# Three instead of two Strassen pairs in the down projection, and evictions of the gated products at high priority

## The chip, the cores and the metric

The kernel runs on one core of one Trainium2 chip. The time is device time in microseconds (us) of one execution; the lower the better. The kernel before takes 1574.93 us, the median of three runs (1574.7 to 1575.7).

## The reference, cut to what matters

One layer of a gated hybrid block on 256 tokens, model width 2048. All matrices are float32.

```
h = rms_norm(x) ; proj = h @ w_in                      # 2048 -> 12288
y_a, y_b, y_x = three branches, each 1024 wide @ (1024 x 2048)
merged = sum_i sigmoid(gate_i) * y_i                   # gates: 2048 columns of proj each
x = x + rms_norm(merged @ w_o)                         # 2048 x 2048
h = rms_norm(x)
f = square(relu(h @ w_up)) @ w_down                    # 2048 -> 8192 -> 2048
x = x + rms_norm(f)
```

The change touches two places: the product with `w_down` (8192 x 2048), and the step `y_i * sigmoid(gate_i)` that follows each branch's output projection.

## The kernel before

**Products in two parts.** Each float32 number is kept as a high part `wh` (or the first half of an activation tile), rounded to fp32r, and a low part `wl` (what the rounding left out). A product is three matmuls: high by high, high by low, low by high. For each weight tile that is loaded into `raw`, ScalarE makes `wh` (L146, L163, or L168 with a gain) and VectorE subtracts to make `wl` (L147, L164, L169). The tiles `raw` have 6 buffers, `wh` and `wl` 5 each; `in_unit` (L197) fetches four units ahead of the one that TensorE works on (`LOOK`, L48).

**Blocks.** `block` (L286) computes 256 tokens by 1024 columns as four banks of 128 x 512, C11, C12, C21 and C22. A plain k-tile of 128 rows of the weight (a unit called row here, R in short) gives four products, 12 matmuls. Two k-tiles can be taken together as a pair by Strassen's scheme (the form with seven products instead of eight): 21 matmuls instead of 24. A pair j comes as four units, first, second, outer and inner (f, s, o and i in short):

- first j is loaded; only its right half is split, for product P1 (3 matmuls). Then GpSimd issues a DMA that adds its left half onto its right half in place (L149).
- second j is loaded and split (6 matmuls). Then GpSimd issues a DMA that adds its left half onto first's left half (L151).
- outer j is made by VectorE from first and second with two additions (L138, L139), which wait for the DMA of L149 and for second's load, and is split (6 matmuls, banks P6 and C21).
- inner j is the tile of first after both DMAs, split again (6 matmuls, banks Q5 and P7).

The activations that go with them are sums of quarters: `quarter_sums` (L644) for the input and `w_o`, `down_sums` (L921) for the down projection. `plan_rows` (L101) interleaves these units with plain rows. With two pairs and `lead=4` (L403) a down block has 20 units:

```
R R R R f0 R s0 R f1 R o0 R s1 i0 R o1 R i1 R R
```

When the last matmul into P1, P6, P7 and Q5 has been issued, `gathered` adds these four banks into the four sums that C11 to C22 stand for (`gather` L335, or `gather_add` L344 where sums of earlier blocks are there).

**Stages.** The MLP goes through 8192 hidden channels in four parts of 2048 (the loop at L930). Each part has four groups of the up projection (`channels_first`, 128 matmuls a group) and then the down projection: two blocks `n` = 0 and 1 of 1024 columns, or in the last part one such block and two `tokens_first` groups of 512 columns without pairs. So seven blocks have pairs. The hidden channels' sums for the pairs (`down_sums`) are made as groups 0 and 1 of the up projection come out.

**Order.** Instructions are placed by the tile framework's scheduler: each has a priority, `fetch` works at an offset of 400 (`PRIO`), `soon()` (L190) at 800; others go at the priority of their place in the text. The result is one fixed sequence on each engine, in which an instruction waits for its semaphores and those behind it wait with it. PSUM has 8 banks; a new bank is taken from those whose last reader comes first in the program.

**The gated products.** `out_of` (L677) multiplies the four banks of a branch's output by the gates (L684 or L686) and adds them up (L687). After the last one, `turn_merged` transposes the sums on TensorE (L791) for the product with `w_o`, whose block g_o[0] has three pairs (R R f0 s0 f1 o0 s1 i0 R f2 ...).

Of the kernel before, what the change touches and what calls it, by code (L numbers as in the profile page):

```python
# [8 lines left out]
F32 = mybir.dt.float32  # L9
# [6 lines left out]
P = 128  # L16
# [10 lines left out]
NC5 = 512  # L27
# [15 lines left out]
X_PAIRS = ((0, 8), (1, 9), (2, 10))  # L43
GATES = ((0, 3), (2, 3), (0, 3))
O_PAIRS = ((0, 4), (1, 5), (2, 6))
D_PAIRS = ((0, 4), (1, 5))
TQ = ((0, 0), (1, 0), (0, 1), (1, 1))
LOOK = 4  # L48
PRIO = 400
# [4 lines left out]
def tile_hybrid_block(ctx, tc, x, head, xT, mem, memT, vecs, w_in, w_a_out, w_b_out, w_kv, w_x_out, w_o,  # L54
# [12 lines left out]
    def name(p):  # L67
        uid[0] += 1
        return f"{p}_{uid[0]}"
# [260 lines left out]
        return acc  # L330

    def t512():
        return sm.tile([P, NC5], F32, tag="u512", name=name("u"), bufs=3)

    def gather(acc, sums):  # L335

# [340 lines left out]
    def out_of(b, n, act, s):  # L677
        acc = block(g_y[b, n], act)
        if b == 2:
            m[n] = t8([P, 2, 2, NC5])  # L680
        for t, q in TQ:
            y, mn, sn = acc[f"C{t + 1}{2 - q}"], m[n][:, q, t, :], s[:, t, q, :]
            if b == 2:
                nc.vector.tensor_tensor(mn, y, sn, ALU.mult)  # L684
            else:
                nc.vector.tensor_tensor(sn, y, sn, ALU.mult)  # L686
                nc.vector.tensor_tensor(mn, mn, sn, ALU.add)  # L687

    def branch(b, act, behind=lambda n: None, amid=lambda n: None):
        for n in range(2):  # L690
# [230 lines left out]
    def down_sums(fd, j, qa, qb):  # L921

        s = t512().rearrange("p (i t) -> p i t", i=4)
        nc.vector.tensor_tensor(s[:, 0, :], qa[:, P:], qb[:, P:], ALU.subtract)
        nc.vector.tensor_tensor(s[:, 1, :], s[:, 0, :], qa[:, :P], ALU.subtract)
        nc.vector.tensor_tensor(s[:, 2, :], qa[:, :P], qa[:, P:], ALU.subtract)
        nc.vector.tensor_tensor(s[:, 3, :], qb[:, :P], s[:, 1, :], ALU.add)
        split(s, fd[:, 0, j], fd[:, 1, j])

    for blk in range(4):  # L930
        f, kept = [], []
        fd = t8([P, 2, len(D_PAIRS), 4, P], F32R)
        for g in range(4):
            first = blk == 0 and g == 0
            if first:
# [17 lines left out]
        if blk == 3:  # L953
            res = [t8([P, D]) for _ in range(2)]
            for t in range(2):
                x2[t] = t8([P, D])
                nc.sync.dma_start(x2[t], x2_kept[t])
        forms = [fd[:, i] for i in range(2)]
        for n in range(2 if blk < 3 else 1):
            def part(t, q):  # L960
                return acc2[t][:, (2 * n + q) * NC5:(2 * n + q + 1) * NC5]

            acc = block(g_dn[blk, n], pair(f), forms,
                        lambda acc: gather(acc, part) if blk == 0 else gather_add(acc, part))
            for t, q in TQ:
                after_down(blk, 2 * n + q, t, acc[f"C{t + 1}{2 - q}"])
# [64 lines left out]
```

## Time and profile before

| | |
|---|---|
| three runs | 1574.7, 1574.93, 1575.7 us |
| profiled execution | 1574.08 us, span of its instructions 1572.2 us |
| PE (TensorE matmul) busy | 1551.4 us, 99% of the span, 7866 instructions |
| DVE (VectorE) busy | 1245.8 us, 79% |
| ACT (ScalarE) busy | 831.5 us, 53% |
| POOL (GpSimd) busy | 55.6 us, 4% |
| chain that ended last | PE 91%, DMA 3%, DVE 3%, issue 2% |
| granted TensorE clock | 0.997 of full speed |

The chain is followed back from the last instruction to what released each step; its shares say which engine's work set the end. A busy PE is a modelled figure, since matmuls are pipelined: two matmuls of 0.39 us each begin 0.227 us apart. So the pace of TensorE is better read from the time between the starts of two stages, divided by the matmuls between them.

### The profile page before, as it was taken

Reading aid. Unit: us, or ns where it says so; the run is one execution under the profiler, and the core shown is the slowest. Engines: PE = TensorE matmul, PEld = TensorE weight load, DVE = VectorE, ACT = ScalarE, POOL = GpSimd, SP = SyncE. Lnnn points to the kernel's source line nnn. Section 1 sums busy time; section 2 is a strip of 40 time slices with the busy share of each in tenths; the row PEclk is TensorE's granted clock in tenths of the full one; section 3 lists DMA queues with packets and bytes.
Section 4 is the critical chain, followed back from the end, with each engine's and each line's share of the span. In section 5 each row is a group of like instructions: output and inputs, shape, how many; then the busy total and the mean of one; then the engine's idle time right before and its main releaser. Section 6 shows DMA issues by size and latency. Waiting matters only on the chain.

```text
span 1572.2 us, 21520 instructions
## 1 busy us (share of the span) xinstructions
PE 1551.4 (99%) x7866; PEld 1324.9 (84%) x7866; DVE 1245.8 (79%) x1883; ACT 831.5 (53%) x1170; POOL 55.6 (4%) x75
## 2 busy tenths in 40 slices
PE   8999999999999999999999999999999999999997
PEld 7888888888888888888788988888888888888886
DVE  7888787798898988778776787778778687777785
ACT  7654454554443545455555665456545555456552
POOL 0000000000000010000100000000000000000000
PEclk9999999999999999999999999999999999999999
DMA  9765555587666768558776665776577666776682
GB/s 321 221 206 190 190 163 172 159 234 223 189 189 174 229 187 286 181 174 237 226 259 196 221 191 175 228 240 191 167 234 232 202 190 199 208 236 189 207 259 81
DMA packets 132521, 324.54 MB, mean 206 GB/s; under 512 B 10432, under 2 KB 14784, under 8 KB 131392
## 3 DMA queue, kind: packets, MB, share of 16 engines
q1 hardware_dynamic: 124352, 308.50, 61.7%
q0 software_dynamic: 8064, 14.68, 5.4%
q8 instruction: 61, 1.00, 0.3%
q14 instruction: 44, 0.36, 0.1%
HBM read 304.26 MB, written 4.19 MB: 196 GB/s over the span
## 4 chain that ended last, share of the span: by engine, by line
PE 91%; DMA 3%; DVE 3%; issue 2%; ACT 0%; POOL 0%; SPq 0%; POOLq 0%; DVEq 0%; ACTq 0%
PE bank L84 90%; DMA raw<-raw 2%; DVE wl L147 1%; DMA raw<-in_w_o 1%; DMA t<-in_xT 0%; DMA raw<-in_w_down 0%; DVE t L833 0%; DVE t L364 0%; DVE raw L139 0%; DVE t L672 0%; PE bank L841 0%; ACT wh L146 0%; DVE t L918 0%; DVE wl L169 0%; DVE t L687 0%
## 5 line engine op out<-in xcount | busy, mean ns | idle before, releaser
L84 PE MATMUL bank<-wh,t 128*128 128x512 f32 (+1 forms) x2536 | 778.2, 387 | 0.0
L84 PEld LDWEIGHTS bank<-wh,t 128*128 128x128 f32 x2536 | 474.0, 188 | 96.6 <-DVE t L364 0.5
L146 ACT CAST wh<-raw 128x1024 fp32r<-128x1024 f32 (+1 forms) x328 | 330.2, 1017 | 330.7 <-PE bank L84 246.0
L84 PE MATMUL bank<-wl,t 128*128 128x512 f32 (+1 forms) x1268 | 490.4, 387 | 0.5 <-DVE wl L147 0.5
L84 PE MATMUL bank<-t,wh 128*128 128x512 f32 (+1 forms) x1936 | 464.5, 391 | 6.0 <-ACT wh L163 4.6
L147 DVE TENSOR_TENSOR wl<-raw,wh 128x1024 fp32r<-128x1024 f32 (+1 forms) x328 | 379.6, 1176 | 95.8 <-ACT wh L146 93.7
L84 PEld LDWEIGHTS bank<-t,wh 128*128 128x128 f32 x1936 | 354.9, 189 | 73.5 <-ACT wh L163 4.6
L84 PEld LDWEIGHTS bank<-wl,t 128*128 128x128 f32 x1268 | 238.2, 188 | 48.8 <-DVE wl L147 1.2
L84 PEld LDWEIGHTS bank<-t,wl 128*128 128x128 f32 x1936 | 248.7, 191 | 10.6 <-DVE wl L164 1.1
L163 ACT CAST wh<-raw 128x1024 fp32r<-128x1024 f32 (+1 forms) x161 | 168.1, 1046 | 165.7 <-PE bank L84 152.6
L164 DVE TENSOR_TENSOR wl<-raw,wh 128x1024 fp32r<-128x1024 f32 (+1 forms) x161 | 195.5, 1217 | 73.7 <-ACT wh L163 73.2
L84 PE MATMUL bank<-t,wl 128*128 128x256 f32 (+1 forms) x1936 | 252.0, 283 | 0.9 <-DVE wl L164 0.9
L169 DVE SCALAR_TENSOR_TENSOR wl<-raw,vec,wh 128x512 fp32r<-128x512 f32 x256 | 180.4, 747 | 46.2 <-ACT wh L168 45.7
L168 ACT ACTIVATE wh<-raw,vec 128x512 fp32r<-128x512 f32 x256 | 171.5, 717 | 76.1 <-PE bank L84 57.0
L596 DVE SCALAR_TENSOR_TENSOR t<-a_pad,vec,t 128x256 f32<-128x256 f32 x240 | 103.9, 482 | 0.0
L359 ACT COPY s<-bank 128x256 f32<-128x256 f32 x128 | 45.6, 368 | 54.6 <-PE bank L84 53.2
L360 DVE TENSOR_TENSOR s<-bank,s 128x256 f32<-128x256 f32 x128 | 51.7, 420 | 19.3 <-ACT s L359 19.3
L149 POOL DMA_DIRECT2D raw<-raw x28 | 24.4, 872 | 1025.3 <-DVE wl L147 1014.5
L363 ACT CAST t<-s 128x256 fp32r<-128x256 f32 x88 | 34.2, 401 | 37.7 <-DVE s L946 29.4
L138 DVE TENSOR_TENSOR raw<-raw,raw 128x512 f32<-128x512 f32 x28 | 19.3, 689 | 28.3 <-DMA raw<-raw 27.1
L364 DVE TENSOR_TENSOR t<-s,t 128x256 fp32r<-128x256 f32 x88 | 36.3, 421 | 5.0 <-ACT t L363 3.8
L151 POOL DMA_DIRECT2D raw<-raw x28 | 24.2, 863 | 127.1 <-DMA raw<-raw 108.8
(144 smaller groups left out, 530.6 us busy)
## 6 DMA issues: line engine op xcount, KB each, us to landing
raw<-in_w_in SPq DMA_DIRECT2D x191, 512.0 KB, 4.3
raw<-in_w_up SPq DMA_DIRECT2D x128, 512.0 KB, 4.0
raw<-in_w_down SPq DMA_DIRECT2D x128, 512.0 KB, 4.8
raw<-in_w_kv SPq DMA_DIRECT2D x32, 512.0 KB, 3.9
raw<-in_w_o SPq DMA_DIRECT2D x32, 512.0 KB, 5.3
raw<-raw POOLq DMA_DIRECT2D x56, 256.0 KB, 3.7
raw<-in_w_x_out SPq DMA_DIRECT2D x16, 512.0 KB, 4.6
raw<-in_w_b_out SPq DMA_DIRECT2D x16, 512.0 KB, 5.3
```

The source lines that it names most:

```text
L84: nc.tensor.matmul(o, a, b, start=start, stop=stop)
L146: nc.scalar.copy(h[:, part], raw[:, part])
L147: pace[0] = nc.vector.tensor_tensor(l[:, part], raw[:, part], h[:, part].bitcast(F32), ALU.subtract).ins
L163: nc.scalar.copy(h, raw)
L164: pace[0] = nc.vector.tensor_tensor(l, raw, h.bitcast(F32), ALU.subtract).ins
L168: nc.scalar.mul(h[:, j, :], raw[:, j, :], g)
L169: pace[0] = nc.vector.scalar_tensor_tensor(l[:, j, :], raw[:, j, :], g, h[:, j, :].bitcast(F32), ALU.mult, ALU.subtract).ins
L359: nc.scalar.copy(t, b[:, T:])
L360: nc.vector.tensor_tensor(dst, b[:, :T], t, ALU.add)
L363: nc.scalar.copy(dst_h, src)
L364: nc.vector.tensor_tensor(dst_l, src, dst_h.bitcast(F32), ALU.subtract)
L596: nc.vector.scalar_tensor_tensor(conv[:, c, :], src, w, conv[:, c, :], ALU.mult, ALU.add)
```

## The change

Three things are changed. `D_PAIRS` has a third pair, k-tiles 2 and 6 of each part. Because of its size, the tile for the pairs' activation sums becomes two tiles (high and low), so that the MLP holds one more of the 13 large buffers; the 512-column scratch tile has two buffers instead of three; the buffers `kept` go with the number of pairs. And the evictions in `out_of` are placed under `soon()`.

```diff
-D_PAIRS = ((0, 4), (1, 5))
+D_PAIRS = ((0, 4), (1, 5), (2, 6))
...
     def t512():
-        return sm.tile([P, NC5], F32, tag="u512", name=name("u"), bufs=3)
+        return sm.tile([P, NC5], F32, tag="u512", name=name("u"), bufs=2)
...
-        for t, q in TQ:
-            y, mn, sn = acc[f"C{t + 1}{2 - q}"], m[n][:, q, t, :], s[:, t, q, :]
-            if b == 2:
-                nc.vector.tensor_tensor(mn, y, sn, ALU.mult)
-            else:
-                nc.vector.tensor_tensor(sn, y, sn, ALU.mult)
-                nc.vector.tensor_tensor(mn, mn, sn, ALU.add)
+        with soon():
+            for t, q in TQ:
+                y, mn, sn = acc[f"C{t + 1}{2 - q}"], m[n][:, q, t, :], s[:, t, q, :]
+                if b == 2:
+                    nc.vector.tensor_tensor(mn, y, sn, ALU.mult)
+                else:
+                    nc.vector.tensor_tensor(sn, y, sn, ALU.mult)
+                    nc.vector.tensor_tensor(mn, mn, sn, ALU.add)
...
-        split(s, fd[:, 0, j], fd[:, 1, j])
+        split(s, fd[0][:, j], fd[1][:, j])
...
-        fd = t8([P, 2, len(D_PAIRS), 4, P], F32R)
+        fd = [t8([P, len(D_PAIRS), 4, P], F32R) for _ in range(2)]
```

The units of a down block with pairs now stand in this order (22 units):

```
R R R R f0 s0 R f1 o0 R s1 i0 R f2 o1 s2 R i1 o2 R i2 R
```

The first place where the instructions' order is shown is on DVE, at the end of the last branch's output (the banks bank_1256, 1258, 1252 and 1257 are its C banks; raw_1275 and raw_1278 are first 0 and second 0 of the block with `w_o`). Before:

```order
L147 TENSOR_TENSOR wl_1277_6910<-raw_1275_6907,wh_1276_6909 128x512
L686 TENSOR_TENSOR t8_1170_6413<-bank_1256_6802,t8_1170_6413 128x512
L147 TENSOR_TENSOR wl_1280_6929<-raw_1278_6926,wh_1279_6928 128x1024
L138 TENSOR_TENSOR raw_1293_6981<-raw_1275_6907,raw_1278_6926 128x512
L687 TENSOR_TENSOR t8_654_3547<-t8_654_3547,t8_1170_6413 128x512
L147 TENSOR_TENSOR wl_1291_6973<-raw_1289_6970,wh_1290_6972 128x512
L139 TENSOR_TENSOR raw_1293_6981<-raw_1293_6981,raw_1278_6926 128x512
L686 TENSOR_TENSOR t8_1170_6413<-bank_1258_6816,t8_1170_6413 128x512
L686 TENSOR_TENSOR t8_1170_6413<-bank_1252_6789,t8_1170_6413 128x512
L687 TENSOR_TENSOR t8_654_3547<-t8_654_3547,t8_1170_6413 128x512 x2
L686 TENSOR_TENSOR t8_1170_6413<-bank_1257_6809,t8_1170_6413 128x512
```

And now (L686 has become L687, and L687 L688):

```order
L147 TENSOR_TENSOR wl_1277_6910<-raw_1275_6907,wh_1276_6909 128x512
L687 TENSOR_TENSOR t8_1170_6413<-bank_1256_6802,t8_1170_6413 128x512
L147 TENSOR_TENSOR wl_1280_6929<-raw_1278_6926,wh_1279_6928 128x1024
L688 TENSOR_TENSOR t8_654_3547<-t8_654_3547,t8_1170_6413 128x512
L687 TENSOR_TENSOR t8_1170_6413<-bank_1258_6816,t8_1170_6413 128x512
L687 TENSOR_TENSOR t8_1170_6413<-bank_1252_6789,t8_1170_6413 128x512
L688 TENSOR_TENSOR t8_654_3547<-t8_654_3547,t8_1170_6413 128x512 x2
L687 TENSOR_TENSOR t8_1170_6413<-bank_1257_6809,t8_1170_6413 128x512
L147 TENSOR_TENSOR wl_1291_6973<-raw_1289_6970,wh_1290_6972 128x512
L688 TENSOR_TENSOR t8_654_3547<-t8_654_3547,t8_1170_6413 128x512
L138 TENSOR_TENSOR raw_1293_6981<-raw_1275_6907,raw_1278_6926 128x512
L139 TENSOR_TENSOR raw_1293_6981<-raw_1293_6981,raw_1278_6926 128x512
```

All evictions now stand ahead of L138, which waits for a DMA.

The second place is on DVE in the middle of a down block (`n` = 0 of the second part). Before, from first 1 to inner 0 (raw_1943 is first 1, raw_1956 second 1):

```order
L147 TENSOR_TENSOR wl_1945_10427<-raw_1943_10424,wh_1944_10426 128x512
L147 TENSOR_TENSOR wl_1949_10438<-raw_1947_10435,wh_1948_10437 128x1024
L147 TENSOR_TENSOR wl_1952_10457<-raw_1950_10453,wh_1951_10456 128x1024
L138 TENSOR_TENSOR raw_1965_10523<-raw_1943_10424,raw_1956_10484 128x512
L147 TENSOR_TENSOR wl_1955_10469<-raw_1953_10466,wh_1954_10468 128x1024
L139 TENSOR_TENSOR raw_1965_10523<-raw_1965_10523,raw_1956_10484 128x512
L147 TENSOR_TENSOR wl_1958_10487<-raw_1956_10484,wh_1957_10486 128x1024
```

And now, from outer 0 to the row behind second 2 (raw_1954 is first 1, raw_1964 second 1, raw_1941 inner 0, raw_1973 first 2, raw_1979 second 2):

```order
L147 TENSOR_TENSOR wl_1959_10465<-raw_1957_10461,wh_1958_10464 128x1024
L147 TENSOR_TENSOR wl_1963_10475<-raw_1961_10472,wh_1962_10474 128x1024
L147 TENSOR_TENSOR wl_1966_10487<-raw_1964_10484,wh_1965_10486 128x1024
L138 TENSOR_TENSOR raw_1976_10542<-raw_1954_10442,raw_1964_10484 128x512
L139 TENSOR_TENSOR raw_1976_10542<-raw_1976_10542,raw_1964_10484 128x512
L147 TENSOR_TENSOR wl_1968_10504<-raw_1941_10382,wh_1967_10503 128x1024
L147 TENSOR_TENSOR wl_1971_10513<-raw_1969_10510,wh_1970_10512 128x1024
L147 TENSOR_TENSOR wl_1975_10526<-raw_1973_10523,wh_1974_10525 128x512
L147 TENSOR_TENSOR wl_1978_10546<-raw_1976_10542,wh_1977_10545 128x1024
L138 TENSOR_TENSOR raw_1989_10595<-raw_1973_10523,raw_1979_10555 128x512
L147 TENSOR_TENSOR wl_1981_10558<-raw_1979_10555,wh_1980_10557 128x1024
L147 TENSOR_TENSOR wl_1986_10573<-raw_1984_10570,wh_1985_10572 128x1024
```

The third L138 stands one instruction behind outer 1's subtraction and right ahead of second 2's.

The third place is on PE at the end of that part's block `n` = 1. Before, the last bank of the block (bank_2003) and the first matmuls of the up projection (banks 2064 to 2067, of which 2067 is the bank that Q5 had):

```order
L84 MATMUL bank_2003_10704<-wh_2047_10917,t8_1914_10309 128x512
L84 MATMUL bank_2064_11017<-t8_1285_6966,wh_2050_10929 128x512
L84 MATMUL bank_2065_11018<-t8_1285_6966,wh_2050_10929 128x512
L84 MATMUL bank_2066_11019<-t8_1285_6966,wh_2050_10929 128x512
L84 MATMUL bank_2067_11020<-t8_1285_6966,wh_2050_10929 128x512
```

Now (2092 is the bank that Q5 had):

```order
L84 MATMUL bank_2022_10751<-wh_2071_10979,t8_1928_10345 128x512
L84 MATMUL bank_2089_11074<-t8_1285_6966,wh_2074_10991 128x512
L84 MATMUL bank_2090_11075<-t8_1285_6966,wh_2074_10991 128x512
L84 MATMUL bank_2091_11076<-t8_1285_6966,wh_2074_10991 128x512
L84 MATMUL bank_2089_11074<-t8_1285_6966,wh_2074_10991 128x512
L84 MATMUL bank_2090_11075<-t8_1285_6966,wh_2074_10991 128x512
L84 MATMUL bank_2091_11076<-t8_1285_6966,wh_2074_10991 128x512
L84 MATMUL bank_2092_11077<-t8_1285_6966,wh_2074_10991 128x512 x2
```

The bank that Q5 had is now written seventh instead of fourth.

## Rows read from the trace of the kernel before

**Rows 1.** The waits of PE: us in total, times, longest us.

```profile
PE bank L791 <- DVE t L687: 1.7, 1, 1.7
...
PE bank L791 <- DVE t L364: 1.0, 1, 1.0
```

**Rows 2.** Windows, second part: up; down n=0; n=1; both. Busy us (instructions), clock, DMA.

```profile
1040.01:1129.07 89.06, 89.06 (x513) 78.69 (x512) 66.35 (x123) 50.18 (x87) 0.00 (x0) 1.00 0.65 195
1129.07:1171.30 42.23, 42.23 (x188) 34.98 (x187) 34.45 (x47) 22.76 (x28) 3.44 (x4) 1.00 0.71 220
1171.30:1213.39 42.09, 42.09 (x187) 34.84 (x186) 32.77 (x40) 21.64 (x25) 3.44 (x4) 1.00 0.73 218
...
1129.07:1213.39 84.32, 84.32 (x373) 69.82 (x372) 67.23 (x86) 44.40 (x53) 6.88 (x8) 1.00 0.72 219
```

**Rows 3.** DVE groups, 1129.07 to 1213.39 us: busy us, mean ns, idle before.

```profile
L147 DVE TENSOR_TENSOR wl<-raw,wh 128x1024 fp32r<-128x1024 f32 x32 | 38.8, 1222 | 11.0 <-ACT wh L146 10.6
...
L138 DVE TENSOR_TENSOR raw<-raw,raw 128x512 f32<-128x512 f32 x4 | 2.8, 689 | 1.5 <-DMA raw<-raw 1.5
L147 DVE TENSOR_TENSOR wl<-raw,wh 128x512 fp32r<-128x512 f32 x4 | 2.8, 689 | 0.9 <-ACT wh L146 0.9
L139 DVE TENSOR_TENSOR raw<-raw,raw 128x512 f32<-128x512 f32 x4 | 2.7, 687 | 0.0
```

**Rows 4.** Line L149, all 28 additions by DMA, from issue to landing.

```profile
DMA to landing us min/median/max: 3.3/4.8/9.1
```

**Rows 5.** Timeline of POOL: start us, us, instruction [idle before <-releaser].

```profile
589.12 0.87 POOL L149 DMA_DIRECT2D raw<-raw  x1 [4.77 <-DMA raw<-in_w_in]
598.27 0.87 POOL L151 DMA_DIRECT2D raw<-raw  x1 [8.28 <-DMA raw<-raw]
...
720.92 0.86 POOL L149 DMA_DIRECT2D raw<-raw  x1 [5.96 <-DVE wl L147]
726.63 0.86 POOL L151 DMA_DIRECT2D raw<-raw  x1 [4.84 <-DMA raw<-raw]
...
1141.80 0.86 POOL L149 DMA_DIRECT2D raw<-raw  x1 [5.74 <-DVE wl L147]
1146.64 0.86 POOL L151 DMA_DIRECT2D raw<-raw  x1 [3.98 <-DMA raw<-raw]
```

**Rows 6.** Timeline of DVE behind the last branch's output.

```profile
765.55 1.22 DVE L147 TENSOR_TENSOR wl<-raw,wh 128x1024 fp32r<-128x1024 f32 x1
769.81 0.69 DVE L138 TENSOR_TENSOR raw<-raw,raw 128x512 f32<-128x512 f32 x1 [3.04 <-DMA raw<-raw]
...
773.43 1.28 DVE L687 TENSOR_TENSOR t<-t,t 128x512 f32<-128x512 f32 x2
```

**Rows 7.** Timeline of PE in the same stretch.

```profile
772.23 0.27 PE L791 MATMUL bank<-ident,t 128*128 128x128 f32 x1
774.17 0.99 PE L791 MATMUL bank<-ident,t 128*128 128x128 f32 x7 [1.67 <-DVE t L687]
...
784.62 0.63 PE L791 MATMUL bank<-ident,t 128*128 128x128 f32 x4 [1.03 <-DVE t L364]
```

**Rows 8.** Timeline at the end of the second part's block n=1.

```profile
1208.22 0.68 DVE L350 TENSOR_TENSOR u<-bank,u 128x512 f32<-128x512 f32 x1
...
1211.28 0.68 DVE L353 TENSOR_TENSOR u<-bank,u 128x512 f32<-128x512 f32 x1
...
1213.39 1.98 PE L84 MATMUL bank<-t,wh 128*128 128x512 f32 x8
```

**Rows 9.** Timeline of the last part's down block.

```profile
1475.05 0.90 SPq L957 DMA_DIRECT2D t<-x_kept  x2
...
1478.01 0.86 POOL L149 DMA_DIRECT2D raw<-raw  x1 [112.95 <-DVE wl L147]
...
1487.24 0.69 DVE L138 TENSOR_TENSOR raw<-raw,raw 128x512 f32<-128x512 f32 x1 [2.72 <-DMA raw<-raw]
...
1499.87 0.50 PE L84 MATMUL bank<-wl,t 128*128 128x512 f32 x1 [0.52 <-DVE wl L147]
```

More of the change, by code (lines that the diff above doesn't have):

```diff
@@ L957, in tile_hybrid_block @@
                 nc.sync.dma_start(x2[t], x2_kept[t])
-        forms = [fd[:, i] for i in range(2)]
         for n in range(2 if blk < 3 else 1):
@@ L961, in part @@
                 return acc2[t][:, (2 * n + q) * NC5:(2 * n + q + 1) * NC5]
-            acc = block(g_dn[blk, n], pair(f), forms,
+            acc = block(g_dn[blk, n], pair(f), fd,
                         lambda acc: gather(acc, part) if blk == 0 else gather_add(acc, part))
```

## The prediction

> **What bounds the kernel now.** I read the table of busy shares first: TensorE is busy 99% of the span at a granted clock of 0.997, and the chain that ended last is 91% TensorE. Its waits come next; outside the start they are few and short [rows 1]. Then the windows by stage: in the second part, both down blocks take 84.32 us for 2 x 186 = 372 matmuls, 226.7 ns apart, with no idle time, at full clock [rows 2]. So a matmul removed in a down block is worth 226.7 ns, as long as VectorE keeps ahead. VectorE is busy 34.45 of 42.23 us in block 0 and 32.77 of 42.09 us in block 1 [rows 2]; no other engine is near. Its waits in these blocks are for ScalarE's `wh` and for the additions by DMA (L138) [rows 3]. The reader is to see two things: TensorE has nothing left to give but its work, and VectorE has 8 to 9 us to spare in a block of 42, but works its list strictly in order.
>
> **The change part by part.**
>
> *Matmuls.* A pair saves 24 - 21 = 3 matmuls, in seven blocks: 21 x 226.7 ns = -4.76 us. By the Trainium skill (TensorE: Matmul & The Clock Gate, Back-to-back issue gap) an isolated matmul of 512 columns at full clock begins 216 ns after the one ahead; the sum would be -4.5 us by it. The rows here show 226.7 ns, so the measured pace is used.
>
> *VectorE's work.* Two plain rows (2 x 1222 ns) go; first (689), second, outer and inner (3 x 1222) and the two additions (689 + 687) come [rows 3]: +3.29 us a block. The load becomes 37.7 of 41.5 us in block 0 and 36.1 of 41.4 us in block 1: hidden on average, by the 7.8 and 9.3 us idle now. `down_sums` runs a third time in each part, four subtractions or additions and one split, under 3.5 us at 0.69 us each; the up projection leaves VectorE 89.06 - 66.35 = 22.7 us idle [rows 2], so I count it as nothing, and if that cover went it would be at most 4 x 3.5 = 14 us. ScalarE gains 1.5 casts a block and stays at little over half.
>
> *Buffers.* Sixth and further loads still find a `raw` buffer as the blocks with three pairs at the input do; the second `fd` tile takes the buffer of tiles whose last reader was the down block before, and the scratch tiles are written in VectorE's own order, mostly. I count nothing.
>
> *The end of the block.* The last inner unit now stands 12 matmuls from the end instead of 24. The chain on VectorE from L350 to the end of L353, which frees Q5's bank, took 1208.22 to 1211.96 = 3.74 us; the up projection began at 1213.39, so 1.4 us were left [rows 8]. That slack would turn into a wait of 0.6 us or so, had the scheduler not moved the first use of Q5's bank from fourth to seventh place (third place of the order). From the last P7 matmul to that use there are now 12 + 6 matmuls, 4.1 us, against 3.74 us and a start that lags by a few tenths: 0 to 0.5 us at each of two ends, and I take 0.1.
>
> *The evictions.* Now: L138 stands ahead of three evictions, waits 3.04 us for its DMA until 769.81, and the sums of L687 come out at 774.7 [rows 6]. TensorE's transposes, begun at 772.23, wait for them until 774.17: 1.94 us between two starts that need 0.11, a loss of 1.8 us [rows 7]. In the new order all L687 and L688 stand ahead of L138. From 766.7, when the subtraction at 765.55 has gone, seven instructions of 0.6 us each run in what was idle time and end near 771.5, ahead of 772.23. So this stall goes. The next one, 1.03 us idle at 784.62 [rows 7] behind a VectorE that is late, may go, too, as VectorE is some 3 us further; against this its three new neighbours (f1, outer 0, second 1) are wanted 1.8 us earlier. Ends: 0 (the wait moves to outer 0) and -3.0; I take -2.4, nearer to the far end, because the idle time of L138 is really filled. The other five `out_of` show no stall now, and the C banks that they wait for are ready in order, so I count nothing for them.
>
> *The wait that is late next.* The new order puts the third L138 ahead of second 2's subtraction (second place of the order). L138 waits until the addition L149 of first 2 has landed. Between first 2 and second 2 TensorE has only first (3) and outer 1 (6 matmuls), 2.0 us. Before, two plain rows and more stood there. When must the DMA have landed? Second 2's low part is wanted 2.0 + 0.23 us after first 2 begins, and needs L138 (0.6 at its place in a dense list) and 1.22 us before. First 2's own `wh` buffer comes free when outer 0 ends, five units earlier: 36 matmuls, 8.2 us ahead of first 2; its cast (0.62), subtraction (0.69) and the issue (0.3) follow. That would leave 8.2 + 2.2 - 1.6 - 1.8 = 7.0 us for the DMA. But VectorE is not free then: the second L138 has itself waited for its DMA. I followed the list by hand with the durations of [rows 3], from the block's begin at 0: first 1's addition is issued at 11.5 (block 0), lands at 16.8 to 17.1; L138, L139, inner 0, row and first 2 take VectorE to 21; the third addition is issued near 21.3. Second 2's low part is wanted at 28.1, so the DMA has 28.1 - 1.8 - 21.3 = 5.0 us. In block 1 it comes out within 0.3 us of this. What do such additions take? 3.3 us at best, 4.8 us in the middle, 9.1 at most [rows 4]; the second one of a down block 4.6 (1141.80 to 0.29 before the next issue), third ones in blocks with three pairs 5.4 and 8.9 [rows 5]. So the wait lies around zero: I take 0.4 us in each of six blocks, 2.4 us.
>
> In the last part the loads of `x_kept`, issued at 1475.05, slow first 0's addition to 9.1 us, VectorE waits until 1487.24, and TensorE loses 0.5 us at 1499.87 [rows 9]. Now L138 stands ahead of two evictions and of second 0, and these loads are issued two units earlier, so they are over sooner. I take +1.1 us, from -0.5 (the old stall gone) to +3. Together the waits are +3.5 us with both ends: -0.5 if all land within 5 us, and 7 x (8.9 - 5.0) = +27 us if all were as slow as the one at 589.12.
>
> *Sum.* -4.76 - 2.4 + 3.5 + 0.2 = -3.5 us. The profiled execution took 1574.08 us (span 1572.2 and 1.9 around it): 1570.6. It lies 0.85 us under the median of the runs, 1574.93, so the forecast for a median is 1571.4 us.
>
> **The rivals.**
>
> *All is hidden.* -4.76, -3.0 and -0.5 for the stall of the last part: -8.3, 1566.6 us. For it: the three-pair blocks at the input and w_o run now without a wait for their third outer unit [rows 1], even with 8.9 us [rows 5]. Against it: they have a plain row between outer 1 and second 2, 2.7 us more.
>
> *The evictions bring nothing.* TensorE then waits for outer 0 or the transposes at the same place, because VectorE's work between 764 and 786 us is the same: -4.76 + 3.7 = -1.1, 1573.9 us. For it: two stalls follow each other within 12 us [rows 7]. Against it: 3.04 us of idle time are filled [rows 6].
>
> *The wait costs what the matmuls save.* 1.0 us in each of the seven blocks, that is an addition of 6.0 us: -4.76 - 2.4 + 7 = about 0, 1574.9 us.
>
> *Slower.* The third L138 in each of the seven blocks holds up second 2's subtraction. From (7.2 + 3.15) / 7 = 1.5 us a block on, additions over 6.5 us, the kernel is slower than can be mistaken; with 7.5 us it is -7.2 + 17.5 = +10.3, 1585 us. The row at 589.12 shows that such a time occurs, the middle of 4.8 us [rows 4] speaks against it as the rule. What could make it so is that weight loads are under way throughout a down block. The Trainium skill (DMA: Bandwidth & Descriptors, Issuing engines are not separate DMA queues) says that transfers issued by any engine end up on the same 16 DMA engines and interleave; by it the addition issued by GpSimd shares them with the loads that SyncE issues, and with a DMA share of 0.72 in these blocks it would not stay near 3.3 us. The 9.1 us beside the loads of `x_kept` agree [rows 9].
>
> **How the numbers follow.** What a measurement of this kernel can tell from no change is about 0.2%, 3.15 us: faster is below 1571.8, slower above 1578.1. Chances: forecast 0.45 (1569 to 1573; two thirds of it faster), all hidden 0.20, evictions bring nothing 0.15 (a little of it faster), wait as dear as the saving 0.15, slower 0.05. So faster 0.53, within 0.42, slower 0.05. The range from 1567.0 to 1576.0 leaves out a part of the best case, the tail of the fourth and the slower one.
>
> **What would show it.** Right: 183 x 2 matmuls in 83.0 us where no wait falls, or 0.3 to 1 us more in the two down blocks of a part, with the loss in PE's waits on `wl` L147 behind a DVE L138 that waits for a DMA; no wait of the transposes (L792) on L688; the stall of the last part between 0 and 3 us. Wrong: two down blocks at over 85 us, stalls at the up projection's begin for a bank, or waits of TensorE in blocks that have none now. The forecast fails if the third addition takes clearly less or more than 5 to 6 us, or if VectorE, at 91% in block 0, falls behind for another reason.

## The result, and the profile after

The changed kernel takes 1594.72 us, the median of four runs (1589.64 to 1596.76), against 1574.82 us for the kernel before on the same chip: 1.0119 times as long, 95% interval 1.0105 to 1.0132. The forecast was 1571.4 us with a range of 1567.0 to 1576.0. The profiled execution is the fastest of the four, 1589.64 us (span 1587.9, mean granted clock 0.996; the three others had 0.992 or 0.993).

PE's waits come first, as in [rows 1]; columns are us in total, times, longest.

```profile
PE bank L84 <- DVE wl L147: 15.8, 7, 3.8
...
PE bank L84 <- DVE u L353: 1.8, 2, 1.3
...
PE bank L84 <- DVE t L364: 0.7, 1, 0.7
```

The transposes' waits of before are gone; TensorE now waits for VectorE's low parts (L147), 15.8 us in seven waits. The windows of the down projection's first three parts (two blocks each) and of the two up projections behind the last two of them show where; columns as in [rows 2], us, then busy us of PE, PEld, DVE, ACT and POOL, clock, DMA share and GB/s:

```profile
954.43:1045.11 90.68, 85.18 (x367) 69.68 (x366) 67.83 (x86) 46.88 (x57) 10.35 (x12) 0.98 0.72 213
1134.18:1218.80 84.62, 83.30 (x367) 68.54 (x366) 69.73 (x90) 46.96 (x57) 10.32 (x12) 1.00 0.77 226
1308.74:1400.45 91.71, 85.13 (x367) 69.74 (x366) 69.20 (x89) 46.77 (x57) 10.35 (x12) 0.98 0.71 209
1218.80:1308.74 89.94, 89.38 (x513) 78.64 (x512) 71.20 (x135) 50.58 (x88) 0.00 (x0) 1.00 0.63 197
1400.45:1491.10 90.65, 89.39 (x513) 78.63 (x512) 71.82 (x136) 50.67 (x88) 0.00 (x0) 1.00 0.68 208
```

Each pair of blocks took 84.3 us before [rows 2]. Now it is 90.68, 84.62 and 91.71: +6.4, +0.3 and +7.4 us, with six matmuls fewer. The up projections (89.06 before) lose 0.9 and 1.6, the last part 0.4, the start 0.6; the branches with the block of `w_o` win 0.5 and the up projection behind them 1.4. Together +15.7 us, the difference of the spans.

One block shows the mechanism. VectorE's timeline from first 2's subtraction on (start us, us, instruction, idle time and its releaser in brackets), then GpSimd's and SyncE's, then TensorE's:

```profile
974.78 0.69 DVE L147 TENSOR_TENSOR wl<-raw,wh 128x512 fp32r<-128x512 f32 x1
976.16 1.23 DVE L147 TENSOR_TENSOR wl<-raw,wh 128x1024 fp32r<-128x1024 f32 x1 [0.69 <-ACT wh L146]
983.72 0.69 DVE L138 TENSOR_TENSOR raw<-raw,raw 128x512 f32<-128x512 f32 x1 [6.34 <-DMA raw<-raw]
984.33 2.35 DVE L147 TENSOR_TENSOR wl<-raw,wh 128x1024 fp32r<-128x1024 f32 x2
```

```profile
971.11 0.86 POOL L151 DMA_DIRECT2D raw<-raw  x1 [4.40 <-DMA raw<-raw]
975.77 0.86 POOL L149 DMA_DIRECT2D raw<-raw  x1 [3.80 <-DVE wl L147]
983.93 0.86 POOL L151 DMA_DIRECT2D raw<-raw  x1 [7.29 <-DMA raw<-raw]
```

```profile
975.39 2.34 SPq L141 DMA_DIRECT2D raw<-in_w_down  x3
```

```profile
982.08 0.61 PE L84 MATMUL bank<-wh,t 128*128 128x512 f32 x2
985.60 0.61 PE L84 MATMUL bank<-wl,t 128*128 128x512 f32 x1 [2.91 <-DVE wl L147]
986.01 1.05 PE L84 MATMUL bank<-wh,t 128*128 128x512 f32 x2
986.87 0.63 PE L84 MATMUL bank<-wl,t 128*128 128x512 f32 x1
...
989.59 0.62 PE L84 MATMUL bank<-wh,t 128*128 128x512 f32 x2
```

The third addition by DMA goes out at 975.77, 21.3 us after the block's begin (954.43), just where the prediction had it. It lands at 983.64, after 7.9 us. Until then L138 holds VectorE, and the subtraction at 984.33, second 2's, comes 3.1 us too late. Six of the seven blocks have such a stall: 3.1, 2.8, 1.5, 4.0, 2.9 and 1.8 us, 16.0 in all. They follow the landing of the third addition, counted from its block's begin, to within 0.1 us: each stall is the landing less 26.1 us (29.2 and 3.1, 28.9 and 2.8, 27.6 and 1.5, 30.1 and 4.0, 29.1 and 2.9, 27.9 and 1.8), and the block without one has the only landing as early as that, 26.1. The whole list of L149 shows the longer additions, against [rows 4]:

```profile
DMA to landing us min/median/max: 3.3/5.4/8.9
```

Behind the stall matmuls begin 0.43 us apart, not 0.227 (two from 986.01 to 986.87). Windows before, in and behind this stretch show the granted clock in the third column from the end: 0.52 is the lower of its two levels, 1.2 GHz.

```profile
978.00:982.30 4.30, 4.30 (x20) 3.57 (x19) 0.00 (x0) 1.84 (x2) 0.00 (x0) 1.00 0.99 277
...
985.70:988.90 3.20, 3.20 (x8) 2.52 (x9) 3.17 (x4) 1.52 (x2) 0.00 (x0) 0.52 0.68 158
989.20:993.00 3.80, 3.80 (x17) 3.12 (x17) 3.23 (x4) 2.43 (x4) 0.00 (x0) 0.99 0.96 357
```

This execution has two such stretches, behind its two longest stalls: 15 matmuls, each about 0.2 us longer, 3.2 us in all.

### The profile page after: what moved, and what is told of

It is laid out like the page before. It is cut to its first block, busy times and chain, and to the rows that moved or that the text cites. A ratio compares the mean times of both kernels' runs of the same rounds, so it can differ in the third digit from the quotient of the medians.

```text
span 1587.9 us, 21599 instructions
## 1 busy us (share of the span) xinstructions
PE 1553.3 (98%) x7845; PEld 1322.8 (83%) x7845; DVE 1266.7 (80%) x1931; ACT 842.1 (53%) x1188; POOL 67.7 (4%) x89
## 4 chain that ended last, share of the span: by engine, by line
PE 76%; DVE 8%; DMA 8%; issue 6%; ACT 1%; POOL 0%; SPq 0%; POOLq 0%; DVEq 0%; ACTq 0%
PE bank L84 76%; DMA raw<-raw 5%; DVE wl L147 4%; DMA raw<-in_w_down 2%; ACT wh L146 1%; DVE wl L169 1%; DVE raw L138 1%; DMA raw<-in_w_in 1%; DVE raw L139 0%; DMA raw<-in_w_o 0%; DMA t<-in_xT 0%; DVE t L911 0%; DVE t L364 0%; DVE t L834 0%; DVE u L353 0%
## 5 line engine op out<-in xcount | busy, mean ns | idle before, releaser
L146 ACT CAST wh<-raw 128x1024 fp32r<-128x1024 f32 (+1 forms) x342 | 338.4, 1008 | 328.8 <-PE bank L84 194.5
L84 PE MATMUL bank<-wl,t 128*128 128x512 f32 (+1 forms) x1261 | 489.9, 389 | 15.9 <-DVE wl L147 15.8
L147 DVE TENSOR_TENSOR wl<-raw,wh 128x1024 fp32r<-128x1024 f32 (+1 forms) x342 | 389.7, 1167 | 78.7 <-ACT wh L146 77.8
L163 ACT CAST wh<-raw 128x1024 fp32r<-128x1024 f32 (+1 forms) x161 | 168.1, 1046 | 163.9 <-PE bank L84 151.3
L164 DVE TENSOR_TENSOR wl<-raw,wh 128x1024 fp32r<-128x1024 f32 (+1 forms) x161 | 195.4, 1217 | 70.2 <-ACT wh L163 69.4
L149 POOL DMA_DIRECT2D raw<-raw x35 | 30.7, 878 | 997.2 <-DVE wl L147 657.5
L138 DVE TENSOR_TENSOR raw<-raw,raw 128x512 f32<-128x512 f32 x35 | 24.2, 691 | 58.5 <-DMA raw<-raw 54.8
L151 POOL DMA_DIRECT2D raw<-raw x35 | 30.2, 863 | 168.5 <-DMA raw<-raw 149.4
L364 DVE TENSOR_TENSOR t<-s,t 128x256 fp32r<-128x256 f32 x84 | 34.7, 421 | 3.1 <-ACT t L363 1.9
```

What stands on the lines that cost most here:

```text
L84: nc.tensor.matmul(o, a, b, start=start, stop=stop)
L138: nc.vector.tensor_tensor(raw[:, 0], a[:, 1], b[:, 0], ALU.add)
L146: nc.scalar.copy(h[:, part], raw[:, part])
L147: pace[0] = nc.vector.tensor_tensor(l[:, part], raw[:, part], h[:, part].bitcast(F32), ALU.subtract).ins
L163: nc.scalar.copy(h, raw)
L164: pace[0] = nc.vector.tensor_tensor(l, raw, h.bitcast(F32), ALU.subtract).ins
```

## The experiments

Theory A: VectorE works in order, the third L138 waits for first 2's addition by DMA, and second 2's low part is held up behind it. Rival B: VectorE has too much work. Rival C: the 14 more transfers slow all loads. Rival D: the evictions' new priority disturbs what follows. The smaller scratch pool and the tile cut in two are in e3, e11 and e12 as well, which are fast, so they are no rivals.

One table for all, since most runs answer to each other. "Seven blocks" is the time of the seven down blocks with pairs, from each one's first matmul to the next one's, in the profiled execution; 1302 matmuls at 226.7 ns are 295.1 us with two pairs, 1281 are 290.4 with three. "Third addition" is the mean over the seven blocks of its issue (us after the block's begin), its duration and its landing. "Branches" is the stage from the start of the first to the end of the last of the 1513 matmuls that end with `w_o`. The executions of one kernel with stalls differ by 3 to 12 us (the changed kernel's by 7), so a difference of a few us between the profiles of two such kernels, which are one execution each, tells nothing.

| run | time us | ratio (95%) | seven blocks | third addition | branches |
|---|---|---|---|---|---|
| before | 1574.1 to 1574.8 | | 295.9 | | 351.1 |
| after | 1594.7 | 1.0119 (1.0105 to 1.0132) | 310.4 | 21.5 + 6.9 = 28.4 | 350.6 |
| e1 pairs alone | 1596.5 | 1.0153 (1.0131 to 1.0174) | 318.7 | 22.1 + 7.0 = 29.1 | 349.6 |
| e2 evictions alone | 1572.5 | 0.9990 (0.9982 to 0.9999) | 296.7 | | 349.1 |
| e3 all additions later | 1567.7 | 0.9961 (0.9949 to 0.9974) | 291.2 | 20.7 + 5.9 = 26.7 | 349.6 |
| e4 lead of two | 1594.3 | 1.0136 (1.0121 to 1.0150) | 316.1 | 19.0 + 6.8 = 25.8 | 351.9 |
| e5 two pairs, later | 1578.0 | 1.0024 (1.0013 to 1.0034) | 295.1 | | 357.1 |
| e6 as e3, old priority | 1573.9 | 0.9999 (0.9990 to 1.0008) | 291.9 | | 354.4 |
| e7 four pairs, later | 1601.0 | 1.0167 (1.0145 to 1.0189) | 320.6 | | 349.6 |
| e8 sums by GpSimd | 1579.7 | 1.0033 (1.0020 to 1.0046) | 294.3 | | 358.3 |
| e9 third pair later | 1588.4 | 1.0091 (1.0074 to 1.0108) | 311.5 | 22.5 + 7.7 = 30.3 | 350.1 |
| e10 third sum by GpSimd | 1575.2 | 1.0003 (0.9993 to 1.0013) | 296.3 | | 349.7 |
| e11 later in the down blocks | 1567.7 | 0.9961 (0.9949 to 0.9973) | 291.1 | 21.2 + 5.1 = 26.3 | 350.6 |
| e12 as e11, old priority | 1569.0 | 0.9967 (0.9955 to 0.9979) | 290.4 | 20.7 + 5.5 = 26.2 | 350.3 |
| e13 seven raw buffers | 1600.0 | 1.0148 (1.0129 to 1.0167) | 324.9 | 22.0 + 7.4 = 29.4 | 353.2 |
| e14 first two pairs later | 1574.7 | 1.0002 (0.9994 to 1.0011) | 296.3 | 20.3 + 5.8 = 26.1 | 348.3 |
| e15 last two pairs later | 1570.6 | 0.9970 (0.9959 to 0.9980) | 294.3 | 21.4 + 5.8 = 27.2 | 349.8 |
| e16 seconds' own buffers | 1598.5 | 1.0153 (1.0139 to 1.0167) | 320.8 | 23.0 + 6.7 = 29.7 | 350.2 |
| e17 e16 and later | 1568.5 | 0.9962 (0.9949 to 0.9976) | 290.5 | 21.0 + 3.9 = 24.9 | 350.2 |
| e18 second's sum by GpSimd | 1613.8 | 1.0246 (1.0229 to 1.0264) | 337.9 | 24.5 + 5.2 = 29.8 | 349.2 |

### The two parts alone (e1, e2)

e1 is the change with the line `with soon():` around the evictions taken out. e2 is the kernel before with that line put in.

> The three pairs alone, with the evictions of the gated products at their old priority. Theory A (VectorE takes its list in order; the third L138 of a block waits for the addition by DMA and holds up second 2's low part): all of the loss is in the down blocks and the evictions are worth the 0.5 us that the stages showed, so the time is that of the changed kernel plus 0.5, about 1595 us. Rival D (the evictions' new priority disturbs what follows): 1570 to 1576 us.

> The evictions at high priority alone, with two pairs. By the stages of the two traces they gain 0.5 us: 1574.4 us. The prediction's term was 2.4 us: 1572.4 us. Rival D (their priority is what costs the time): above 1580 us.

All the loss comes with the third pair: e1 is at least as slow as the changed kernel. The evictions alone gain 1.6 us (0.2 to 2.8), and nothing of the loss is theirs.

### The place of the additions (e3, e4)

e3 puts L138 and L139 behind the last subtraction that the program has written so far (`pace[0]`); e4 leaves them and changes the order of the units:

```diff
-            nc.vector.tensor_tensor(raw[:, 0], a[:, 1], b[:, 0], ALU.add)
-            nc.vector.tensor_tensor(raw[:, 1], raw[:, 0], b[:, 1], ALU.add)
+            with tc.issue_after(pace[0]):
+                nc.vector.tensor_tensor(raw[:, 0], a[:, 1], b[:, 0], ALU.add)
+                nc.vector.tensor_tensor(raw[:, 1], raw[:, 0], b[:, 1], ALU.add)
```
```diff
-                g_dn[blk, n] = plan_rows(w_down, blk * D, n * 2 * NC5, KD, D_PAIRS, lead=4)
+                g_dn[blk, n] = plan_rows(w_down, blk * D, n * 2 * NC5, KD, D_PAIRS, lead=2)
```

> The changed kernel with the two additions L138 and L139 placed in VectorE's list behind the last subtraction that stands ahead of them in the program, so that second 2's subtraction goes first. The same work on every engine and the same transfers. Theory A: the stalls at second 2 go, and with them the time at the low clock behind them; 1574.8 - 4.8 for the matmuls - 0.5 for the evictions, + 1 to 2 for the waits of banks at the up projections' begin: 1570 to 1572 us. Rival B (VectorE has too much work, 91% of a block): the same subtractions and additions must still be done, so 1585 us or more. Rival C (the 14 more transfers slow the loads): 1590 us or more.

> The changed kernel with two plain rows at a down block's begin instead of four; the two others come to stand between outer 1 and second 2 and at the block's end. The third addition by DMA then has 2.7 us more before second 2's low part is wanted. Theory A with transfers of 6 to 8 us as in the changed kernel's trace: at most 0 to 1 us of stall a block is left, and the end of the block has its slack back: 1568 to 1574 us. Rivals B and C (too much work on VectorE, transfers in each other's way): the work and the transfers are the same, so within 5 us of the changed kernel's time.

e3 has the same work and the same transfers, and takes 1567.7 us: 6.4 less than the kernel before beside it, and by the two ratios 25 less than the changed kernel. Its first pair of blocks, whose window has the columns of those above, is full:

```profile
956.74:1039.70 82.96, 82.96 (x368) 68.72 (x366) 67.35 (x85) 46.15 (x57) 10.34 (x12) 1.00 0.81 232
```

So VectorE does not have too much work, and 14 more additions do not slow the loads as such; rivals B and C fall. e4 missed theory A's expectation and came out as B and C had it. The row between outer 1 and second 2 helps nothing, because the scheduler places the third L138 one unit further ahead as well, in front of that row's subtraction. VectorE's timeline in e4:

```profile
1152.92 3.19 DVE L147 TENSOR_TENSOR wl<-raw,wh 128x1024 fp32r<-128x1024 f32 x3
1162.68 0.69 DVE L138 TENSOR_TENSOR raw<-raw,raw 128x512 f32<-128x512 f32 x1 [6.57 <-DMA raw<-raw]
1163.29 1.22 DVE L147 TENSOR_TENSOR wl<-raw,wh 128x1024 fp32r<-128x1024 f32 x1
```

So another order of the units does not help while L138 moves along with it on VectorE.

### Where the later place helps, and how far pairs go (e5 to e8)

e5 is the kernel before with e3's edit. e6 is e3 without `soon()`. e7 is e3 with a fourth pair:

```diff
-D_PAIRS = ((0, 4), (1, 5), (2, 6))
+D_PAIRS = ((0, 4), (1, 5), (2, 6), (3, 7))
```

e8 is the changed kernel with both additions by DMA made by GpSimd (below the first; the other is alike):

```diff
-            nc.gpsimd.dma_start(raw[:, 1], raw[:, 0], accum_op=ALU.add)
+            nc.gpsimd.tensor_tensor(raw[:, 1], raw[:, 1], raw[:, 0], ALU.add)
```

> The kernel before (two pairs, evictions at their old priority) with L138 and L139 behind the subtractions that stand ahead of them in the program, to separate what the new place is worth by itself. If it only takes away waits for the addition by DMA: the two stalls there are behind an L138 that waits (1.8 us at the transposes, 0.5 to 0.7 in the last part) go, 1572 to 1573 us. Rival (the new place gains by itself, and the third pair little): 1569 us or less.

> Three pairs with the later additions, evictions at the old priority. If the evictions' gain came from going ahead of an L138 that waits, nothing is left of it once L138 goes behind them anyway: 1567 to 1568.5 us, as with the new priority. If the priority is a gain of its own: 1.5 to 2.5 us above that, 1569 to 1570 us.

> A fourth pair, k-tiles 3 and 7, on top of the three with later additions. 21 fewer matmuls, -4.8 us if all else is hidden: 1563 us. VectorE's load in a block becomes about 41.0 us against 360 / 2 matmuls of 226.7 ns = 40.8 us, so if the load bounds, a block loses 0.5 to 2 us: 1566 to 1577 us. I expect the load to show: 1569 us.

> The changed kernel with its order, but with the two additions that were DMAs (L149 and L151) as additions on GpSimd. Theory A: what held VectorE up is the 5 to 8 us of the third addition; GpSimd has it done in 1 to 2 us, L138 no longer waits, and the time is 1569 to 1573 us although the order and VectorE's load are those of the changed kernel. Rival B (VectorE's load): 1585 us or more. That GpSimd's additions and VectorE's hold each other up could add 1 to 5 us.

e5 and e6 missed. In the down blocks they do what e3 does (295.1 and 291.9), but at the transposes it goes worse than before. TensorE's waits in e5, and ScalarE's timeline there:

```profile
PE bank L792 <- DVE t L365: 4.1, 1, 4.1
```

```profile
785.53 1.04 ACT L147 CAST wh<-raw 128x1024 fp32r<-128x1024 f32 x1 [4.46 <-DMA raw<-in_w_o]
786.48 0.58 ACT L364 CAST t<-bank 128x512 fp32r<-128x512 f32 x1
```

[Rows 1] has 1.0 us for that wait. A cast whose weights come late now stands ahead of L364, which empties the transposes' banks. In e3, with the evictions at high priority, two of these L364 stand ahead of such a cast, and TensorE has no wait there. So the later place is safe in the down blocks, and in the block of `w_o` only with the new priority.

e7 lost 26 us where 6 of gain were expected, and not by VectorE's load: in one part's two blocks it is busy 69.7 of 88.8 us. ScalarE's casts wait for the second addition (L140 here) 112.9 us in all, in e11 61.9:

```profile
ACT wh L147 <- DVE raw L140: 112.9, 39, 5.4
```

With four pairs the chain from a DMA to two additions, a cast and a subtraction comes too often for the units between. e8 missed, too (1579.7). Its blocks come to 294.3, 16 us under the changed kernel at the same order: without the long third addition four blocks lose 1 us each and three nothing. The rest of its time went elsewhere: the branches take 358.3 us, and VectorE is busier at the same work (74.0 us in the first part's blocks, 67.35 in e3), as it and GpSimd hold each other up (last section).

### One place, one sum, and the two priorities (e9 to e12)

e9 is e3's edit for `w is w_down and j == 2` alone, e11 for `w is w_down`, e12 is e11 without `soon()`. In e10 GpSimd makes first 2's sum alone:

```diff
-            nc.gpsimd.dma_start(raw[:, 1], raw[:, 0], accum_op=ALU.add)
+            if w is w_down and j == 2:
+                nc.gpsimd.tensor_tensor(raw[:, 1], raw[:, 1], raw[:, 0], ALU.add)
+            else:
+                nc.gpsimd.dma_start(raw[:, 1], raw[:, 0], accum_op=ALU.add)
```

> The changed kernel with only the third pair's L138 and L139 in the down blocks placed later: behind second 2's subtraction and the two behind it. On VectorE nothing else moves but a few of the same block's sums by one place. Theory A says that these seven places are the whole loss: the blocks take 83.0 to 83.7 us for a part's two instead of 91, and the time is 1568 to 1571 us. If any other wait of the changed kernel counts (second L138, banks, priorities), it stays above 1580 us.

> The changed kernel with its order, and in the down blocks only first 2's addition made by GpSimd as an addition instead of a DMA. Theory A: the third L138 keeps its place ahead of second 2's subtraction, but what it waits for comes 5 to 7 us earlier: a part's two blocks take 83 to 84.1 us and the time is 1569 to 1573 us. If it was the place in the list itself or VectorE's load: 1585 us or more.

> The later additions in all the down blocks, and the old place in the blocks at the input and with w_o, where the later place cost 1.6 us at 588.04 us with three pairs and 5.9 us in the kernel with two. With the down blocks of the run in which all additions stand later (83.1 to 83.7 us a part) and the branches of the changed kernel (350.6 us) it is 1567 to 1569 us. If the third additions alone are what counts, the same as with these alone moved.

> The same with the evictions at their old priority: the evictions' term by itself, in a kernel without the stall. With two pairs they gained 1.6 us (0.2 to 2.8): 1.5 to 2.5 us above the run with the new priority, 1569 to 1571 us. If the 6 us between the two priorities with all additions later hold here too: 1573 to 1574 us.

e10 came out above its expectation, but takes away 14 of the 20 us that the blocks lose, by shortening seven sums, with L138 at its place. What is left has another cause, in VectorE's waits:

```profile
DVE raw L138 <- DMA raw<-in_w_down: 22.3, 7, 3.8
```

The third L138 now waits for second 2's load, which went out late, too. e9's blocks take as long as the changed kernel's (311.5 and 310.4 us); the claim that seven places are the whole loss fell. In e9 the stall at second 2 is gone, but second 2's load and the third sum still come late, and ScalarE, VectorE and TensorE follow one another through second 2, the row and outer 2. ScalarE in e9:

```profile
1019.34 1.82 ACT L146 CAST wh<-raw 128x512 fp32r<-128x512 f32 x2 [1.35 <-DVE raw L138]
1027.16 1.05 ACT L146 CAST wh<-raw 128x1024 fp32r<-128x1024 f32 x1 [6.00 <-DMA raw<-in_w_down]
```

e11 and e12 came out as expected. They are the best versions, with e3 and e17: 0.39% and 0.33% faster than before, all within each other's intervals. In e12's trace the seven blocks take 290.4 us, 1281 matmuls without a gap. Between e11 and e12 the evictions' priority makes 1.3 us, less than the intervals can tell.

### Why the third sum and the load come late (e13 to e18)

The rows above have the reason. At 975.25 second 1's addition (L151, issued at 971.11) lands, and at 975.39 and 975.82 SyncE sends two loads that it held; the third of the line above leaves at 977.41. The first of them is second 2's: it goes into the buffer that second 1 had, and L151 reads that one last. In all seven blocks it leaves 0.1 us behind that landing. So two loads of 512 KB and the third addition start within 0.4 us of each other. e13 has seven raw buffers instead of six (`RAW = 7`, with room from other stages' small tiles); e16 has five and two of the seconds' own:

```diff
-            raw = wp.tile([P, 2, NC5], F32, tag="raw", name=name("raw"), bufs=RAW)
+            raw = wp.tile([P, 2, NC5], F32, tag="sec" if what == "second" else "raw", name=name("raw"),
+                          bufs=2 if what == "second" else RAW)
```

e17 is e16 with e11's edit. e14 and e15 are e3's edit for `w is w_down and j < 2` and `j > 0`. e18 is the changed kernel with L151 in the down blocks made by GpSimd.

> The changed kernel with seven raw buffers instead of six (room for it from the small tiles: five instead of six of 128x256, one instead of two of two others, which serve other stages); the order on VectorE in the down blocks is kept. Reading 2 (loads without a free buffer are released together with the third addition and slow it): loads go out earlier, the third addition takes 5 to 6 us instead of 6.9, and the stalls shrink to 0 to 1.5 us a block: 1572 to 1582 us. Reading 1 (the place in the list is what counts, whatever the loads do): 1588 to 1597 us.

> The changed kernel with the additions of pairs 0 and 1 in the down blocks placed later, and the third pair's left ahead of second 2's subtraction. Reading 2: VectorE no longer loses time at the first two, the loads are spread, the third addition goes out some 1 us earlier and takes 5 to 6 us; a stall of 0 to 1.5 us a block is left: 1568 to 1578 us. Reading 1: the third L138 waits as before, 1586 to 1595 us.

> The changed kernel with the additions of pairs 1 and 2 in the down blocks placed later, the first pair's left. The first L138 waits 1.2 us a block in the changed kernel's trace; if that alone doesn't matter, the time is that of all three moved, 1567 to 1570 us. If it delays all that follows as the second did in e9: 1575 to 1588 us.

> The kernel with seven raw buffers (e13), two of them kept for the seconds: second 2's load goes into second 0's buffer, whose addition by DMA is long over, and no load of a down block waits for second 1's. VectorE's order in the down blocks is word for word that of the changed kernel and of e13. If the chain from second 1's addition to the load is what makes the third addition slow, it takes 4 to 6 us and the stalls are 0 to 1 us a block: 1568 to 1578 us. If VectorE's order alone decides: 1588 us or more, as e13.

> The same with the later additions in the down blocks. With both the load's wait and L138's gone nothing is left to gain in the down blocks, which already take 83.1 us a part in e11: 1566 to 1569 us. Below 1565 us something outside the down blocks gains from the seconds' own buffers.

> The changed kernel with L151 in the down blocks as an addition on GpSimd; order on VectorE, buffers and L149 (still a DMA) as in the changed kernel. If the loads that wait for second 1's addition are what slows the third one, the loads go out some 2 to 3 us earlier, the third addition takes 5 to 6 us instead of 6.9, the stalls are 0 to 1.5 us a block, and the time is 1570 to 1581 us. If the place of the third L138 decides whatever the loads do: 1586 to 1597 us.

e14 tells most. Its third L138 stands ahead of second 2's subtraction as in the changed kernel; only the first two pairs' additions were moved. SyncE's and VectorE's timelines in its first block:

```profile
970.14 1.47 SPq L141 DMA_DIRECT2D raw<-in_w_down  x2
```

```profile
977.69 0.69 DVE L138 TENSOR_TENSOR raw<-raw,raw 128x512 f32<-128x512 f32 x1 [2.08 <-DMA raw<-raw]
```

The loads leave 2.0 and 0.9 us ahead of the third addition (issued at 972.15). The first leaves 0.5 us before second 1's addition lands, so in this order it no longer waits for it. The third addition goes out at 20.3 us into the block, less delayed by the L138s ahead of it, and takes 5.8 us on average (5.4 to 6.1). It lands 2.3 us earlier than in the changed kernel, and 0.84 us a block is left: (296.3 - 290.4) / 7.

e15 moves the last two pairs' additions and gets nearly as far: 294.3 us in the blocks, 1570.6 us, 0.6 above its first range. e17 came out as expected; with one load 2 to 4 us ahead and at most one behind, the third addition takes 3.9 us, but no time was left to win.

e13 and e16 missed: more buffers do not help by themselves. In e16 the wait moved to the load of the next block's second in SyncE's list, and the loads behind it came in a bunch again; in e13, too, three loads go out from 981.10 on, 0.3 us ahead of the third addition. e18 shows both sides. SyncE and GpSimd in its first block:

```profile
974.57 1.34 SPq L141 DMA_DIRECT2D raw<-in_w_down  x2
```

```profile
977.59 0.87 POOL L149 DMA_DIRECT2D raw<-raw  x1 [4.45 <-DVE wl L147]
```

With the loads 3.0 and 2.0 us ahead in every block, the third addition takes 5.2 us on average (4.0 to 6.6) in the changed kernel's own order, against 6.9: the bunch is what made it slow. But the time is the worst of all, since the sums on GpSimd wait for longer second additions (6.4 us on average, 5.6 in the changed kernel) and hold VectorE up, so that the third one is issued at 24.5. What the stall would be with the old order, early loads and nothing else changed was not measured.

So three things make the loss: how long the third sum takes, where the L138s stand, and when second 1's addition and the loads behind it let the third sum begin. The sum alone was shortened in e10, which wins 14.1 us in the blocks. The places were moved in groups: the third pair's alone wins nothing (e9), the first two 14.1 (e14), the last two 16.1 (e15), all three 19.3 (e11). The second pair's place is in every group that helps; by itself it was not run, and in e14 the release of the loads changed along with the places. How much each of the two is worth alone stays open.

## Why the prediction was wrong, step by step

**Matmuls, -4.76 us: right.** 295.1 against 290.4 us with no gap (e5, e12).

**VectorE's work counted at nothing: right.** e12 does all of it, and no down block of its trace is more than 0.04 us over its matmuls.

**Buffers counted at nothing: wrong in the mechanism.** That every load finds a buffer was not the question; it is whose buffer, and who reads it last. This step fed the next one. Yet more buffers did not help by themselves (e13, e16).

**The third L138 at 0.4 us a block: the step that failed.** The place was right, and so was its time of issue: 21.3 us by hand, 21.5 measured. The allowance nearly holds as well: 21.3 + 5.0 = 26.3 us into the block, where the stalls say 26.1. The duration was the mis-sized term: 5.4 us, taken from second additions and from the better of two third ones, where it is 6.9 (5.0 to 8.0). So the third sum lands at 28.4 instead of 26.7, and the stall is 2.3 us a block instead of 0.4, 16.0 in all instead of 2.4 + 1.1. The prediction had named the sign, a third addition that takes clearly more than 5 to 6 us.

The rows of before had a part of the key: the price of an addition depends on what starts beside it. There it takes 3.3 us alone, and the seven second additions of the down blocks, with two loads mostly 1 to 3 us ahead, 4.6 to 6.7, on average 5.7; the one that the prediction read, 4.6, is the shortest of them. Two loads that both start in the microsecond before an addition don't occur in the down blocks of before; in the changed kernel and the experiments such an addition takes 6.2 to 8.7 us. To forecast a third one meant following SyncE's list as closely as VectorE's. The Trainium skill (DMA: Bandwidth & Descriptors, Issuing engines are not separate DMA queues) was named in the prediction for just this, transfers of all issuers on the same 16 engines; the trace agrees (7.9 us beside three loads, 3.3 alone). I gave the rival that goes with it a chance of 0.05.

**The clock: not in the prediction.** Of the 20.0 us that the blocks lose (310.4 - 290.4) the stalls are 16.0 and the two stretches at the lower level 3.2; the rest, 0.8, is spread over single matmuls. Executions with a mean clock of 0.992 or 0.993 took 4 to 7 us more; that these are more such stretches is likely, but only the first was profiled.

**The end of the block, 0.2 us: 1.8 instead.** The waits for L353 are 0.6 and 1.3 us in the up projections of the third and fourth part. The order of banks alone does not make them: in e11, with the same end of a block, PE has no wait for L353. That VectorE, late by the stall, makes them is likely, since they go with the stalls.

**The evictions, -2.4 us: right in kind, too large.** The stall at the first transposes goes in every kernel with the new priority. Measured are 1.6 us alone (0.2 to 2.8), and 0.5 in the stage in the changed kernel's profile. The wait that was taken as 1.8 us depends on a DMA in one execution: e12, with the old priority, has in PE's waits

```profile
PE bank L792 <- DVE t L688: 0.9, 1, 0.9
```

And the next stall did not go: TensorE waits 0.76 us for L147 and 0.71 for L364 at 786 us, where [rows 7] has 1.03 at 784.62.

**The last part, +1.1 us: 0.4.** The old stall [rows 9] went, a stall of 1.8 us at second 2 came, and the matmuls save 0.7.

**The rivals.** The slower one had the mechanism and a price: 1585 us at 7.5 us an addition. It came at 6.9 us an addition, with 1589.6 us in the profile, where the clock and the waits for banks came on top, and 1594.7 as the median.

## What to carry to other kernels

A wait in front of other work on an in-order engine is priced by the latest landing of what it waits for; so list what else is started by the same event before taking a median of such transfers. When a stall on one engine's list is moved, look at who made the waited-for thing late: moving the waiter alone (e9) won back 4 us by the ratios and nothing in the profiled blocks, moving it with the two before it 25. A cheap way to use the third pair is to put the additions behind the subtractions that are ready, in the down blocks (e11): 1567.7 us, 0.4% under the kernel before.

## What the runs showed of the hardware

- An addition by DMA of 256 KB from one on-chip tile onto another takes 3.3 us alone and up to 8.9 us beside loads (L149 in the changed kernel). Its time goes with how closely loads start before it: 5.2 us on average with two loads 2.0 and 3.0 us ahead (e18), 6.2 to 8.7 with two in the microsecond before it (the changed kernel and the experiments).
- Behind stalls of 3.1 and 4.0 us TensorE ran at a granted clock of 0.52 and 0.50 for 3.2 us, behind those of 2.8 and 2.9 us it did not. The length of the stall does not settle it: in e18 a stall of 2.6 us (up to 1032.25) was followed by a granted clock of 0.50, in e4 one of 3.05 us (up to 1343.10) by 1.00.
- An addition on GpSimd and one on VectorE at the same time cost VectorE 1.1 us: in e18 L138 takes 1.82 us beside GpSimd's sum (L152 there), else 0.69. It is the later one that pays: at 959.12, where VectorE began 0.06 us ahead, L138 took 0.69 us and GpSimd's sum 1.79. GpSimd's and VectorE's timelines:

```profile
971.85 1.28 POOL L152 TENSOR_TENSOR raw<-raw,raw 128x512 f32<-128x512 f32 x1 [5.29 <-DMA raw<-raw]
```

```profile
971.87 1.82 DVE L138 TENSOR_TENSOR raw<-raw,raw 128x512 f32<-128x512 f32 x1 [0.76 <-DMA raw<-raw]
```

By the Trainium skill (SBUF — State Buffer, SBUF: two separate sides) the two engines share one pair of ports for such instructions, held for a whole instruction while the other waits; 1.82 is near 0.69 plus most of GpSimd's 1.28, and the trace agrees.
